# Modulation in eight products of 1024 columns, and four PSUM banks in the output projection and the early gates of a two-layer encoder

## The chip, the cores and the metric

The kernel runs on one core of a Trainium2 chip. What is measured is the time in device microseconds of one execution. Before the change it is 3258.42 us, the median of three runs (3254.71 to 3266.62 us). Five engines work side by side: TensorE (PE, with its weight loads shown apart as PEld), VectorE (DVE), ScalarE (ACT), GpSimd (POOL) and SyncE (SP), which here only starts transfers. Each works through its own list of instructions in order and waits for others by semaphores. Matrix products accumulate in PSUM banks; everything else lies in SBUF.

## What is computed

Two layers over 1024 tokens of width 1024, in float32. Each layer is a token mixer followed by a gated MLP with a short convolution. Six vectors of 1024 (shift, scale and gate for each half of a layer) come from the conditioning vector c; this is the modulation:

```python
c_act = jax.nn.silu(c)
for l in range(DEPTH):                               # 2 layers
    mod = (c_act @ w_mod[l] + b_mod[l])[:, None, :]  # w_mod[l]: 1024 x 6144
    sh1, sc1, g1, sh2, sc2, g2 = jnp.split(mod, 6, axis=-1)
    h = rms_norm(x, norm_g[l, 0]) * (1 + sc1) + sh1
    parts = jnp.split(h @ w_in[l], split_idx, axis=-1)
    ...                                              # four mixers A, B, C, D
    y = jnp.concatenate([oa, ob, oc, od], axis=-1) @ w_out[l]
    x = x + g1 * rms_norm(y, norm_g[l, 1])
    h = rms_norm(x, norm_g[l, 2]) * (1 + sc2) + sh2
    u = dwconv3(h @ w_up[l], ffn_conv[l])            # 1024 -> 2 x 2816
    ug, uv = jnp.split(u, 2, axis=-1)
    y = (jax.nn.gelu(ug, approximate=True) * uv) @ w_down[l]
    x = x + g2 * rms_norm(y, norm_g[l, 3])
```

## The kernel before

Activations lie transposed, with features on the 128 partitions and tokens along the free axis; the two token halves (512 each) are handled one after the other where PSUM asks for it. Every float32 operand is split into a high and a low part (ACT rounds, DVE or POOL subtracts, L110 and L111), and a product is made of three matmuls, high by high, high by low, low by high (mm3, L525 to L527). A program orders the instructions on each engine by the dependences and by the order of the code, and `issue_after` adds such an edge.

A layer runs through these stages.

- **Mixer**: projections and the four attention groups. PE is the busiest engine there; the change does not touch it.
- **Output projection** (`project_out`, L1149 to L1186). For each half of the tokens eight output tiles m, each 8 contraction tiles by three matmuls, into one PSUM bank of 128x512 and from there by ACT to y (L1173). After the first half, `between` puts in the residual and the MLP's input for that half (norm sums, modulated values on DVE and ACT, split). The second half takes all its banks from the pool pj, which has two.
- **Early gates** (`begin_early`, L1228): the part of six gate products that needs only the first half of the tokens, made while DVE, ACT and POOL bring the second half through its residual and norm. `begin` (L1215) makes eight plus four matmuls, ACT copies the bank out (L1221), twelve more are added to the same bank, and ACT copies again (L1225). All banks come from pj. The weight sums of the first two steps of the up projection (`sums`, L1236) are DVE work beside it.
- **Up projection** (`dense_up`, L1264): 22 steps, each with a convolution on DVE (L944, L946), a GELU on ACT (L1328), a product (L1329), and a store to `actd`. The four tiles ta, tb, tc, tn of the pool t4 hold the convolution's operands here.
- **Down projection** (`dense_down`, L1367). `whole` takes contraction tiles in groups of n (2 or 4), and for each of eight output tiles m makes 2 halves x n x 3 matmuls into a po tile (1024 columns) or two psc banks; DVE adds them to y (L1428). In the first group ACT copies instead. `some` does the last contraction tiles by token halves, 512 columns each (L1435).
- **Layer end**: norm sums, residual, and the next layer's modulated input.

The modulation of the first layer's last gate and five of the second layer's six vectors is a generator (`modulate`, L369) stepped by `advance` (L376). One step loads 128x512 of w_mod into one of two buffers (tag mr, L359) and adds its product with one column of c_act to an accumulator of 128x512 (tag mc, L362 or L364); 16 steps and a fold (`mod_fold`: two transposes, two reductions and some ten small instructions, L418 to L441) make one vector. Six such jobs are stepped in layer 0: 16 steps in the up projection (one per convolution step from the seventh on), 70 in the whole groups (three per m in groups of four, one in groups of two, none in the first group), and the 16 that are left over when `some` begins. In layer 1 the last gate is made in the whole groups.

Of the kernel before, what the change touches and what calls it, by code (L numbers as in the profile page):

```python
# [21 lines left out]
KT = 8  # L22
# [70 lines left out]
class Trunk:  # L93
# [252 lines left out]

    def mod_pieces(self, l, j, room=None):

        nc = self.nc
        accs = []  # L350
        for u in range(2):
            acc = room[u] if room else self.mc.tile([128, 512], F32, name="mc", tag="mc")
            for k in range(KT):
                if room:
                    w = room[2 + (8 * u + k) % (len(room) - 2)]
                else:
                    w = self.mr.tile([128, 512], F32, name="mr", tag="mr")
                at = 1024 * j + 512 * u
                nc.sync.dma_start(w, self.a["w_mod"][l, 128 * k:128 * k + 128, at:at + 512])  # L359
                s = self.cact[:, k:k + 1]  # L360
                if k == 0:
                    nc.vector.tensor_scalar(acc, w, s, None, op0=ALU.mult)  # L362
                else:
                    nc.vector.scalar_tensor_tensor(acc, w, s, acc, op0=ALU.mult, op1=ALU.add)  # L364
                yield
            accs.append(acc)
        return l, j, accs, 0

    def modulate(self, jobs):  # L369

        for l, j in jobs:
            part = yield from self.mod_pieces(l, j)
            self.mod_fold(part, self.mr.tile([128, 512], F32, name="mr", tag="mr"))
            yield

# [130 lines left out]
    def residual(self, y, l, g, hs, xsrc, dst, temp, adders=None, rs=None):  # L506
# [3 lines left out]
        for k in range(KT):  # L510
# [6 lines left out]
            nc.vector.scalar_tensor_tensor(yk, yk, self.col(l, g, k), rs, op0=ALU.mult, op1=ALU.mult)  # L517
            (nc.gpsimd if k % 2 else nc.vector).tensor_add(yk, yk, x)
            (nc.sync if dst is self.a["out"] else nc.scalar).dma_start(dst[128 * k:128 * k + 128, hs], yk)
# [357 lines left out]
    def modulations(self, l):  # L877

        tiles = [self.sp.tile([128, 2048], F32, name="room", tag=t) for t in ("s10", "s11")]
        room = [t[:, at:at + 512] for t in tiles for at in range(0, 2048, 512)]  # L880
        for j in (2, 4, 3):
            pieces = self.mod_pieces(l, j, room)
            try:
                while True:
                    next(pieces)
            except StopIteration as done:
                part = done.value
            yield
            self.mod_fold(part, room[2])
# [215 lines left out]
    def mixer(self, l):  # L1105
        tc, nc = self.tc, self.nc
        with ExitStack() as e:
# [29 lines left out]
            if l == 0:  # L1137
                self.mods = ExitStack()
                self.mc, self.mr = (p(n, 2, self.mods, side="right") for n in ("mc", "mr"))
            self.qlc, kls, rt, self.sc = self.open_shared(f"hmid{l}")  # L1140
# [4 lines left out]
    def project_out(self, l, y, between):  # L1145
        nc = self.nc
        order = ORDER_MIX
        with self.tc.tile_pool(name=f"wo{l}", bufs=1, reuse_waits="tile") as wo:
# [33 lines left out]
            for m in (2, 3, 4, 5, 0, 1, 6, 7):  # L1182
                products(1, (m,), (pj,), False)
                if m == 0:
                    between[1]()
# [28 lines left out]

    def begin(self, u, w1, between=None):  # L1215

        nc = self.nc
        b11, b21 = ([(self.hh[i][:, HALVES[0]], self.hl[i][:, HALVES[0]]) for i in range(k, k + 4)] for k in (0, 4))
        x = self.pj.tile([128, 512], F32, name="pj", tag="pj")
        self.quarter(x, w1, 0, b11)  # L1220
# [6 lines left out]
    def begin_early(self, l, ws):  # L1227

        nc, done = self.nc, []
        for t in range(self.ahead):  # L1230
            u = self.t4.tile([128, 1026], F32, name="u", tag=("tc", "tn")[t % 2])
            done.append(self.begin(u, ws[t] if t < len(ws) else self.up_weight(l, t)))
            nc.scalar.dma_start(self.kept[128 * t:128 * t + 128, :], u[:, 1:1025])
# [30 lines left out]
    def dense_up(self, l, early):  # L1264
# [10 lines left out]
        with tc.tile_pool(name=f"ux{l}", bufs=2, reuse_waits="tile") as ux, \  # L1275
# [79 lines left out]
            for t in range(2, FT):  # L1355
# [7 lines left out]
                gated(t, p.tail())  # L1363
                if t >= ahead:
                    self.advance(1)

    def dense_down(self, l, y, end):  # L1367
# [3 lines left out]
        with tc.tile_pool(name=f"dq{l}", bufs=4, reuse_waits="tile") as dq:  # L1371
# [3 lines left out]
            if last:  # L1375
                self.mc, self.mr = (right.enter_context(tc.tile_pool(name=f"{n}{l}", bufs=2, reuse_waits="tile",
                                                                     side="right")) for n in ("mc", "mr"))
                self.pieces = self.modulate([(l, 5)])
            pools = {"f": (self.fw, "uh", "ul"), "w": (self.w, "wh", "wl"), "q": (dq, "qh", "ql"), "p": (dp, "ph", "pl")}
# [33 lines left out]
            def whole(ops, first):  # L1413
                for m in range(8):
                    if m and not first:
                        self.advance(1 if len(ops) < 4 else 3)
                    if m % 3 < 2:
# [50 lines left out]
    def run(self):  # L1468
# [48 lines left out]
        for l in range(DEPTH):  # L1517
# [8 lines left out]
            with tc.tile_pool(name=f"fw{l}", bufs=3, reuse_waits="tile") as self.fw:  # L1526
                self.project_out(l, y, token_half(0, t))
                self.turn = cycle((0, 0, 0, 1, 1))
                self.pieces = self.modulate([(0, 5), (1, 1), (1, 0), (1, 2), (1, 4), (1, 3)] if l == 0 else [])
                with tc.tile_pool(name=f"te{l}", bufs=1, reuse_waits="tile") as self.te:  # L1530
                    early = [self.up_weight(l, t) for t in range(5)]
                    with tc.tile_pool(name=f"bd{l}", bufs=1, reuse_waits="tile", side="right") as bd:
                        t = self.temps(bd, x="few")
                        token_half(1, t)[0]()
                        done = self.begin_early(l, early)
                        early = [self.sums(l, k, False, self.t4) for k in range(2)]
                        self.dense_input(y, l, 1, t, adders[1], done)
# [91 lines left out]
```

## Time and profile before

| | before |
|---|---|
| median of three runs | 3258.42 us |
| profiled execution | 3276.93 us |
| its span in the trace | 3275.2 us |
| PE busy | 2909.4 us, 89% of the span |
| DVE busy | 2339.0 us, 71% |
| ACT, POOL busy | 1185.3 us, 36%; 1151.7 us, 35% |
| mean clock granted to PE | 0.95 of full speed |

PE is the engine to watch: where it waits, the time grows, and where it does not wait, other engines' work is hidden beside it. The share of each is an average over stages, so the stages are read apart. In layer 0 the output projection and early gates lie at 838 to 940 us of the span, the up projection from 1040 to 1390, the down projection's whole groups up to 1588 and its halves to 1670; in layer 1 the same stages begin at 2450, 2660 and 3000 us.

### The profile page before, as it was taken

Reading aid. Unit: us, or ns where it says so; the run is one execution under the profiler, and the core shown is the slowest. Engines: PE = TensorE matmul, PEld = TensorE weight load, DVE = VectorE, ACT = ScalarE, POOL = GpSimd, SP = SyncE. Lnnn points to the kernel's source line nnn. Section 1 sums busy time; section 2 is a strip of 40 time slices with the busy share of each in tenths; the row PEclk is TensorE's granted clock in tenths of the full one; section 3 lists DMA queues with packets and bytes.
Section 4 is the critical chain, followed back from the end, with each engine's and each line's share of the span. In section 5 each row is a group of like instructions: output and inputs, shape, how many; then the busy total and the mean of one; then the engine's idle time right before and its main releaser. Section 6 shows DMA issues by size and latency. Waiting matters only on the chain. (4 is left out here: it accounts for less than half of the span.)

```text
span 3275.2 us, 35394 instructions
## 1 busy us (share of the span) xinstructions
PE 2909.4 (89%) x13178; PEld 2299.8 (70%) x13178; DVE 2339.0 (71%) x3168; ACT 1185.3 (36%) x1702; POOL 1151.7 (35%) x797
## 2 busy tenths in 40 slices
PE   7888988988888999999888998898897799999897
PEld 3677767776656777777656787677675578877786
DVE  6687567697669778857776736578964797776456
ACT  4232443554443333321233333435534333334121
POOL 1221133224444444542332212242334445456131
PEclk8998999999999999999998999999998899999998
DMA  5235111102333222355531121110133232224323
GB/s 201 72 99 180 58 34 32 54 20 77 127 111 109 87 90 90 119 190 175 169 129 47 57 76 55 37 46 20 52 109 117 83 110 77 78 84 159 105 90 103
DMA packets 122680, 305.32 MB, mean 93 GB/s; under 512 B 13403, under 2 KB 32091, under 8 KB 122508
## 3 DMA queue, kind: packets, MB, share of 16 engines
q1 hardware_dynamic: 113868, 284.19, 26.5%
q10 hardware_dynamic: 8640, 18.88, 1.5%
q8 instruction: 103, 1.69, 0.2%
q14 instruction: 69, 0.57, 0.1%
HBM read 244.38 MB, written 62.03 MB: 94 GB/s over the span
## 5 line engine op out<-in xcount | busy, mean ns | idle before, releaser
L111 POOL TENSOR_TENSOR wl<-raw,wh 128x1024 fp32r<-128x1024 f32 (+2 forms) x82 | 203.3, 2481 | 470.5 <-ACT wh L110 273.0
L534 PE MATMUL pj<-hh,wh 128*128 128x512 f32 x800 | 329.4, 412 | 15.7 <-DVE ql L583 8.4
L535 PE MATMUL pj<-hl,wh 128*128 128x512 f32 x800 | 325.4, 407 | 10.2 <-POOL hl L461 6.4
L538 PE MATMUL pj<-hh,wl 128*128 128x512 f32 x800 | 208.8, 400 | 0.0
L534 PEld LDWEIGHTS pj<-hh,wh 128*128 128x128 f32 x800 | 155.6, 194 | 56.7 <-issue 15.6
L535 PEld LDWEIGHTS pj<-hl,wh 128*128 128x128 f32 x800 | 154.8, 194 | 52.3 <-POOL hl L461 10.2
L946 DVE SCALAR_TENSOR_TENSOR ta<-u,par,ta 128x1024 f32<-128x1024 f32 x88 | 154.9, 1761 | 34.2 <-ACT ta L942 34.1
L538 PEld LDWEIGHTS pj<-hh,wl 128*128 128x128 f32 x800 | 152.5, 192 | 35.5 <-issue 0.9
L698 PE MATMUL po<-s,v 128*96 128x128 f32 (+3 forms) x672 | 133.5, 363 | 44.1 <-ACT s L695 44.0
L698 PE MATMUL po<-hp,v 128*96 128x256 f32 x512 | 126.5, 403 | 37.1 <-ACT hp L695 36.7
L698 PEld LDWEIGHTS po<-s,v 128*96 128x96 f32 x672 | 101.3, 190 | 71.6 <-ACT s L695 54.7
L111 POOL TENSOR_TENSOR ul<-raw,uh 128x1024 fp32r<-128x1024 f32 x45 | 117.2, 2607 | 95.9 <-ACT uh L110 95.6
L110 ACT ACTIVATE wh<-raw 128x1024 fp32r<-128x1024 f32 (+2 forms) x90 | 94.1, 1045 | 154.5 <-PE pj L535 74.3
L581 ACT ACTIVATE qh<-pj 64x512 fp32r<-64x512 f32 x128 | 107.2, 838 | 98.4 <-PE pj L538 52.9
L583 DVE TENSOR_TENSOR ql<-pj,qh 64x512 fp32r<-64x512 f32 x64 | 55.4, 866 | 116.0 <-ACT qh L581 115.3
L946 DVE SCALAR_TENSOR_TENSOR tb<-u,par,tb 128x1024 f32<-128x1024 f32 x88 | 137.3, 1560 | 0.0
L698 PEld LDWEIGHTS po<-hp,v 128*96 128x96 f32 x512 | 85.9, 173 | 72.2 <-ACT hp L695 45.1
L111 POOL TENSOR_TENSOR pl<-raw,ph 128x1024 fp32r<-128x1024 f32 x26 | 67.9, 2612 | 178.0 <-issue 102.9
L364 DVE SCALAR_TENSOR_TENSOR mc<-mr,cact,mc 128x512 f32<-128x512 f32 x98 | 98.1, 1001 | 45.1 <-DMA mr<-in_w_mod_dram 44.7
L565 DVE TENSOR_TENSOR ks<-pj,ks 64x512 fp32r<-64x512 f32 x56 | 51.2, 914 | 108.7 <-ACT ks L564 108.0
L1428 DVE TENSOR_TENSOR y<-y,po 128x1024 f32<-128x1024 f32 x60 | 72.7, 1216 | 69.5 <-PE po L527 69.4
L685 PE MATMUL psc<-qh,ks 128*128 128x256 f32 (+2 forms) x272 | 88.2, 339 | 36.9 <-DVE s L813 15.2
(618 smaller groups left out, 8935.2 us busy)
## 6 DMA issues: line engine op xcount, KB each, us to landing
mr<-in_w_mod_dram SPq DMA_DIRECT2D x144, 256.0 KB, 3.1
raw<-in_w_up_dram SPq DMA_DIRECT2D x56, 512.0 KB, 3.7
raw<-in_w_in_dram SPq DMA_DIRECT2D x52, 512.0 KB, 3.4
raw<-in_w_down_dram SPq DMA_DIRECT2D x50, 512.0 KB, 3.7
actd<-ta SPq DMA_DIRECT2D x44, 512.0 KB, 2.6
uh<-in_w_up_dram SPq DMA_DIRECT2D x26, 512.0 KB, 3.8
room<-in_w_mod_dram SPq DMA_DIRECT2D x48, 256.0 KB, 3.8
xd<-y ACTq DMA_DIRECT2D x48, 256.0 KB, 4.0
```

The costliest lines, as they stand in the source:

```text
L110: self.nc.scalar.activation(hi, src, AF.Copy)
L111: (eng or self.nc.gpsimd).tensor_sub(lo, src, hi.bitcast(F32))
L364: nc.vector.scalar_tensor_tensor(acc, w, s, acc, op0=ALU.mult, op1=ALU.add)
L534: nc.tensor.matmul(ps, wh[:, ks], self.hh[k][:, hs], start=k == 0, stop=False, skip_group_check=True)
L535: nc.tensor.matmul(ps, wh[:, ks], self.hl[k][:, hs], start=False, stop=False, skip_group_check=True)
L538: nc.tensor.matmul(ps, wl[:, ks], self.hh[k][:, hs], start=False, stop=k == KT - 1, skip_group_check=True)
L581: nc.scalar.activation(self.perm(qh[h][o:o + 64], r)[:, n * half:n * half + n, :], src, AF.Copy)
L583: nc.vector.tensor_sub(lo, src, own.bitcast(F32))
L685: nc.tensor.matmul(ps, ks[:, c], qh[:, q0:q1], start=first, stop=False, skip_group_check=True)
L698: nc.tensor.matmul(o[0:96, co], v(tt, h), s[:, cs], start=co.start // 512 not in seen, stop=False, skip_group_check=True)
L946: nc.vector.scalar_tensor_tensor(o, t[:, i:i + n], cw(i), o, op0=ALU.mult, op1=ALU.add)
L1428: self.mark = nc.vector.tensor_add(d, d, p)
```

## The change

Five edits in one. The modulation runs in eight products of 1024 columns per vector instead of sixteen of 512, with one accumulator of 1024 columns, and its loads (512 KB instead of 256 KB) go into the four t4 tiles ta, tb, tc, tn, so the two mr buffers are gone. Up projection steps no longer advance it; its generator is made in the down projection, and a group of four advances it twice per m rather than three times. The second half of the output projection takes odd m from pj and even m from psc. The early gates alternate between pj and psc too. And the two early weight sums are ordered behind the last addition that the second half's residual makes on DVE.

```diff
-    def modulate(self, jobs):
+    def modulate(self, jobs, acc):
+        nc = self.nc
+        tags = cycle("abcn")
         for l, j in jobs:
-            part = yield from self.mod_pieces(l, j)
-            self.mod_fold(part, self.mr.tile([128, 512], F32, name="mr", tag="mr"))
-            yield
+            for k in range(KT):
+                w = self.tmp(next(tags))
+                nc.sync.dma_start(w, self.a["w_mod"][l, 128 * k:128 * k + 128, 1024 * j:1024 * j + 1024])
+                s = self.cact[:, k:k + 1]
+                if k == 0:
+                    nc.vector.tensor_scalar(acc, w, s, None, op0=ALU.mult)
+                else:
+                    nc.vector.scalar_tensor_tensor(acc, w, s, acc, op0=ALU.mult, op1=ALU.add)
+                yield
+            self.mod_fold((l, j, (acc[:, 0:512], acc[:, 512:1024]), 0), self.tmp(next(tags))[:, :512])
...
-            (nc.gpsimd if k % 2 else nc.vector).tensor_add(yk, yk, x)
+            if k % 2:
+                nc.gpsimd.tensor_add(yk, yk, x)
+            else:
+                self.added = nc.vector.tensor_add(yk, yk, x)
...
-                products(1, (m,), (pj,), False)
+                products(1, (m,), (pj if m % 2 else psc,), False)
...
-        x = self.pj.tile([128, 512], F32, name="pj", tag="pj")
+        x = (self.pj if bank == "pj" else self.psc).tile([128, 512], F32, name="x", tag=bank)
...
-            done.append(self.begin(u, ws[t] if t < len(ws) else self.up_weight(l, t)))
+            done.append(self.begin(u, ws[t] if t < len(ws) else self.up_weight(l, t), None, ("pj", "psc")[t % 2]))
...
                 gated(t, p.tail())
-                if t >= ahead:
-                    self.advance(1)
...
-                self.mc, self.mr = (right.enter_context(tc.tile_pool(name=f"{n}{l}", bufs=2, reuse_waits="tile",
-                                                                     side="right")) for n in ("mc", "mr"))
-                self.pieces = self.modulate([(l, 5)])
+                self.mc = right.enter_context(tc.tile_pool(name=f"mc{l}", bufs=1, reuse_waits="tile", side="right"))
+            self.pieces = self.modulate([(l, 5)] if last else [(0, 5), (1, 1), (1, 0), (1, 2), (1, 4), (1, 3)],
+                                        self.mc.tile([128, 1024], F32, name="mc", tag="mc"))
...
-                        self.advance(1 if len(ops) < 4 else 3)
+                        self.advance(1 if len(ops) < 4 else 2)
...
-                        early = [self.sums(l, k, False, self.t4) for k in range(2)]
+                        with self.queued(added):
+                            early = [self.sums(l, k, False, self.t4) for k in range(2)]
```

With 6 x 8 = 48 steps and 49 advances in layer 0's whole groups, all products and folds of layer 0 now lie there; nothing is left over for `some`.

How the order moves, at three places. First DVE in layer 0's first group of four contraction tiles. L362 and L364 are the products before (mc<-mr), L375 and L377 those after (mc<-ta, tb, tc, tn), L1428 and L1429 the additions to y. Before:

```order
L1428 TENSOR_TENSOR y<-y,psc 128x512
L364 SCALAR_TENSOR_TENSOR mc<-mr,cact,mc 128x512
L111 TENSOR_TENSOR ul<-ul,uh 128x1024
L364 SCALAR_TENSOR_TENSOR mc<-mr,cact,mc 128x512
L1428 TENSOR_TENSOR y<-y,psc 128x512
L364 SCALAR_TENSOR_TENSOR mc<-mr,cact,mc 128x512 x3
L1428 TENSOR_TENSOR y<-y,po 128x1024
L364 SCALAR_TENSOR_TENSOR mc<-mr,cact,mc 128x512 x2
L362 TENSOR_SCALAR mc<-mr,cact 128x512
L1428 TENSOR_TENSOR y<-y,po 128x1024
L364 SCALAR_TENSOR_TENSOR mc<-mr,cact,mc 128x512 x2
L1428 TENSOR_TENSOR y<-y,psc 128x512
```

After:

```order
L1429 TENSOR_TENSOR y<-y,po 128x1024
L377 SCALAR_TENSOR_TENSOR mc<-tc,cact,mc 128x1024
L377 SCALAR_TENSOR_TENSOR mc<-tn,cact,mc 128x1024
L1429 TENSOR_TENSOR y<-y,psc 128x512 x2
L377 SCALAR_TENSOR_TENSOR mc<-ta,cact,mc 128x1024
L111 TENSOR_TENSOR ul<-ul,uh 128x1024
L377 SCALAR_TENSOR_TENSOR mc<-tb,cact,mc 128x1024
L1429 TENSOR_TENSOR y<-y,po 128x1024
L377 SCALAR_TENSOR_TENSOR mc<-tc,cact,mc 128x1024
L377 SCALAR_TENSOR_TENSOR mc<-tn,cact,mc 128x1024
L1429 TENSOR_TENSOR y<-y,po 128x1024
```

Two products of 1024 columns now stand between the additions of two neighbouring m where three of 512 stood.

Second, DVE in layer 1's down projection, where the one job there is folded (L418 to L441 before, L423 to L446 after). Before:

```order
L418 STREAM_TRANSPOSE mr<-mc 128x512
L419 TENSOR_REDUCE sm<-mr 128x16
L418 STREAM_TRANSPOSE mr<-mc 128x512
L419 TENSOR_REDUCE sm<-mr 128x16
L421 COPY sm<-sm 64x32
L422 TENSOR_TENSOR sm<-sm 64x32
L423 COPY sm<-sm 32x32
L424 TENSOR_TENSOR sm<-sm 32x32
L426 COPY sm<-sm 32x8 x4
L432 TENSOR_TENSOR mod<-sm,par 128x8
L441 TENSOR_TENSOR gm<-mod,par 128x8
L1428 TENSOR_TENSOR y<-y,po 128x1024 x3
```

After:

```order
L1429 TENSOR_TENSOR y<-y,po 128x1024
L423 STREAM_TRANSPOSE ta<-mc 128x512
L424 TENSOR_REDUCE sm<-ta 128x16
L423 STREAM_TRANSPOSE ta<-mc 128x512
L1429 TENSOR_TENSOR y<-y,psc 128x512
L424 TENSOR_REDUCE sm<-ta 128x16
L426 COPY sm<-sm 64x32
L427 TENSOR_TENSOR sm<-sm 64x32
L428 COPY sm<-sm 32x32
L429 TENSOR_TENSOR sm<-sm 32x32
L431 COPY sm<-sm 32x8 x4
L1429 TENSOR_TENSOR y<-y,psc 128x512
```

The whole fold stood in one piece ahead of the next addition of a po tile; now additions stand within it.

Third, PE in layer 1's early gates (L1208, L1209, L1212 before; L1211, L1212, L1215 after; hx and hp are halves of the input, uh, ul, wh, wl split weights). Before, from the end of one gate's first part into the next:

```order
L1212 MATMUL pj<-hp,ul 128x512
L1208 MATMUL pj<-hp,uh 128x512 [waits Activation_49]
L1209 MATMUL pj<-hp,uh 128x512
L1208 MATMUL pj<-hp,uh 128x512
L1209 MATMUL pj<-hp,uh 128x512
L1208 MATMUL pj<-hx,uh 128x512
L1209 MATMUL pj<-hx,uh 128x512
```

After:

```order
L1215 MATMUL x<-hx,ul 128x512
L1215 MATMUL x<-hp,ul 128x512
L1211 MATMUL x<-hx,wh 128x512
L1212 MATMUL x<-hx,wh 128x512
L1211 MATMUL x<-hp,wh 128x512
L1212 MATMUL x<-hp,wh 128x512
```

...and, after the first matmuls of a further gate,

```order
L1212 MATMUL x<-hp,wh 128x512
L1215 MATMUL x<-hx,wl 128x512
L1211 MATMUL x<-hp,uh 128x512 [waits Activation_49]
L1212 MATMUL x<-hp,uh 128x512
L1211 MATMUL x<-hp,uh 128x512
L1212 MATMUL x<-hp,uh 128x512
```

The matmuls that wait for ACT's copy (pj<-hp,uh, now x<-hp,uh) now stand behind the first parts of two further gates (8+4 and 8+1 matmuls, 21 in all).

## Rows read from the trace of the kernel before

**Rows 1.** Page, busy time of each engine over the span.
```profile
PE 2909.4 (89%) x13178; PEld 2299.8 (70%) x13178; DVE 2339.0 (71%) x3168; ACT 1185.3 (36%) x1702; POOL 1151.7 (35%) x797
```

**Rows 2.** Windows by stage: us; PE, PEld, DVE, ACT, POOL busy; PEclk, DMA share, GB/s.
```profile
2450.00:2562.00 112.00, 82.88 (x293) 58.78 (x291) 53.22 (x82) 44.79 (x71) 43.65 (x31) 0.87 0.39 129
1062.00:1388.00 326.00, 313.12 (x1332) 249.96 (x1332) 267.86 (x251) 117.92 (x146) 161.80 (x123) 0.99 0.28 96
2685.00:2999.00 314.00, 310.07 (x1331) 250.56 (x1332) 242.87 (x235) 118.28 (x146) 159.61 (x123) 0.99 0.25 87
1402.00:1588.00 186.00, 167.38 (x701) 135.58 (x700) 135.58 (x174) 36.86 (x40) 67.11 (x29) 0.94 0.56 180
```

**Rows 3.** Waits of PE, 838 to 940 us: total, times, longest.
```profile
PE pw L525 <- ACT y L1173: 7.2, 2, 6.1
PE po L1348 <- ACT hx L110: 6.6, 1, 6.6
PE pj L1208 <- ACT u L1221: 4.0, 2, 2.5
```

**Rows 4.** Waits of PE, 2450 to 2562 us.
```profile
PE pj L1208 <- ACT u L1221: 10.0, 1, 10.0
PE pw L525 <- ACT y L1173: 8.8, 2, 5.9
```

**Rows 5.** Timeline of ACT, 861 to 879 us: start, duration, instruction, idle before.
```profile
869.29 1.06 ACT L1173 ACTIVATE y<-pw 128x512 f32<-128x512 f32 x2
...
877.56 0.60 ACT L1173 ACTIVATE y<-pw 128x512 f32<-128x512 f32 x1 [6.27 <-PE pw L527]
```

**Rows 6.** Windows of 7 us before and after one of PE's gaps.
```profile
1440.00:1447.00 7.00, 7.00 (x32) 5.80 (x31) 4.10 (x6) 1.06 (x1) 0.09 (x1) 1.00 0.49 147
...
1453.00:1460.00 7.00, 7.00 (x22) 5.53 (x22) 5.42 (x16) 0.87 (x1) 0.00 (x0) 0.67 0.70 228
```

**Rows 7.** GELU of the up projection, layer 0.
```profile
L1328 ACT ACTIVATE ta<-ta x17: 1048/1062/1064, 1061.7 to 1388.2; 128x1024 f32<-128x1024 f32 x17
```

**Rows 8.** GELU of the up projection, layer 1.
```profile
L1328 ACT ACTIVATE ta<-ta x17: 1049/1061/1065, 2684.7 to 2999.1; 128x1024 f32<-128x1024 f32 x17
```

**Rows 9.** Waits of PE in layer 0's whole groups, 1402 to 1588 us.
```profile
PE po L525 <- DVE y L1428: 18.6, 5, 6.5
```

**Rows 10.** Timeline of DVE, 1444 to 1454 us.
```profile
1447.91 1.97 DVE L364 SCALAR_TENSOR_TENSOR mc<-mr,cact,mc 128x512 f32<-128x512 f32 x1 [0.80 <-DMA mr<-in_w_mod_dram]
...
1451.26 1.21 DVE L1428 TENSOR_TENSOR y<-y,po 128x1024 f32<-128x1024 f32 x1
```

**Rows 11.** Lines of DVE, 1402 to 1588 us: busy, mean ns, idle before.
```profile
L364 DVE SCALAR_TENSOR_TENSOR mc<-mr,cact,mc 128x512 f32<-128x512 f32 x56 | 54.2, 968 | 29.9 <-DMA mr<-in_w_mod_dram 29.7
...
L362 DVE TENSOR_SCALAR mc<-mr,cact 128x512 f32<-128x512 f32 x8 | 8.7, 1082 | 1.8 <-DMA mr<-in_w_mod_dram 1.6
```

**Rows 12.** Durations (min/median/max) of a product, 512 columns.
```profile
L364 DVE SCALAR_TENSOR_TENSOR mc<-mr,cact,mc x98: 736/751/2892, 1106.0 to 3055.4; 128x512 f32<-128x512 f32 x98
```

**Rows 13.** Durations of the same operation on 1024 columns, in the convolution.
```profile
L946 DVE SCALAR_TENSOR_TENSOR ta<-u,par,ta x88: 1269/1274/3474, 982.5 to 2995.7; 128x1024 f32<-128x1024 f32 x88
```

**Rows 14.** Waits of PE, 1588 to 1670 us, layer 0's `some`.
```profile
PE pd L525 <- DVE y L1435: 7.2, 4, 2.5
```

**Rows 15.** Timeline of DVE, 3055 to 3070 us, layer 1.
```profile
3056.07 0.70 DVE L418 STREAM_TRANSPOSE mr<-mc 128x512 f32<-128x512 f32 x1
...
3065.08 2.35 DVE L1428 TENSOR_TENSOR y<-y,po 128x1024 f32<-128x1024 f32 x2
```

**Rows 16.** Waits of SP's queue, 1402 to 1588 us.
```profile
SPq L359 <- DVE mc L364: 59.0, 49, 3.5
```

**Rows 17.** Page: POOL's split of a loaded weight; that load, KB, us to landing.
```profile
L111 POOL TENSOR_TENSOR pl<-raw,ph 128x1024 fp32r<-128x1024 f32 x26 | 67.9, 2612 | 178.0 <-issue 102.9
...
raw<-in_w_down_dram SPq DMA_DIRECT2D x50, 512.0 KB, 3.7
```

More of the change, by code (lines that the diff above doesn't have):

```diff
@@ L345, in rotary, with mod_sum @@
                 nc.sync.dma_start(self.csd[:, 512 * i:512 * i + 512], cs)
-    def mod_pieces(self, l, j, room=None):
+    def mod_sum(self, l, j, room):
         nc = self.nc
@@ L351, in mod_pieces @@
         for u in range(2):
-            acc = room[u] if room else self.mc.tile([128, 512], F32, name="mc", tag="mc")
+            acc = room[u]
             for k in range(KT):
[L354 to L357, printed above, removed]
+                w = room[2 + (8 * u + k) % (len(room) - 2)]
                 at = 1024 * j + 512 * u
@@ L364, in mod_pieces @@
                     nc.vector.scalar_tensor_tensor(acc, w, s, acc, op0=ALU.mult, op1=ALU.add)
-                yield
             accs.append(acc)
         return l, j, accs, 0
-    def modulate(self, jobs):
+    def modulate(self, jobs, acc):
+        nc = self.nc
+        tags = cycle("abcn")
         for l, j in jobs:
-            part = yield from self.mod_pieces(l, j)
-            self.mod_fold(part, self.mr.tile([128, 512], F32, name="mr", tag="mr"))
-            yield
+            for k in range(KT):
[8 more added lines that the diff above has]
+            self.mod_fold((l, j, (acc[:, 0:512], acc[:, 512:1024]), 0), self.tmp(next(tags))[:, :512])
     def advance(self, n):
@@ L881, in modulations @@
         for j in (2, 4, 3):
[L882 to L887, printed above, removed]
+            part = self.mod_sum(l, j, room)
             yield
@@ L1138, in mixer @@
                 self.mods = ExitStack()
-                self.mc, self.mr = (p(n, 2, self.mods, side="right") for n in ("mc", "mr"))
+                self.mc = p("mc", 1, self.mods, side="right")
             self.qlc, kls, rt, self.sc = self.open_shared(f"hmid{l}")
@@ L1213, in quarter, with begin @@
         return mm
-    def begin(self, u, w1, between=None):
+    def begin(self, u, w1, between=None, bank="pj"):
         nc = self.nc
         b11, b21 = ([(self.hh[i][:, HALVES[0]], self.hl[i][:, HALVES[0]]) for i in range(k, k + 4)] for k in (0, 4))
-        x = self.pj.tile([128, 512], F32, name="pj", tag="pj")
+        x = (self.pj if bank == "pj" else self.psc).tile([128, 512], F32, name="x", tag=bank)
         self.quarter(x, w1, 0, b11)
@@ L1528, in run @@
                 self.turn = cycle((0, 0, 0, 1, 1))
-                self.pieces = self.modulate([(0, 5), (1, 1), (1, 0), (1, 2), (1, 4), (1, 3)] if l == 0 else [])
                 with tc.tile_pool(name=f"te{l}", bufs=1, reuse_waits="tile") as self.te:
@@ L1534, in run @@
                         token_half(1, t)[0]()
+                        added = self.added
                         done = self.begin_early(l, early)
-                        early = [self.sums(l, k, False, self.t4) for k in range(2)]
+                        with self.queued(added):
+                            early = [self.sums(l, k, False, self.t4) for k in range(2)]
                         self.dense_input(y, l, 1, t, adders[1], done)
```

## The prediction

> **What bounds the kernel now.** I first read the busy time per engine: PE works 89% of the span [rows 1], so time can only be won where PE waits or runs at a lower clock. Second came the windows by stage [rows 2]. In layer 1's output projection and early gates PE is busy 82.9 of 112 us. In layer 0's whole groups of the down projection it is busy 167.4 of 186 us, and DVE 135.6. In layer 0's up projection it is busy 313.1 of 326 us, and in layer 1's, which is the same work without the modulation's steps, 310.1 of 314. Third came PE's waits in these stages. In both layers the second half of the output projection waits for ACT to empty a bank (7.2 and 8.8 us), the early gates wait for ACT's first copy (4.0 and 10.0 us), and the transition ends with 6.6 us of waiting for the input's second half [rows 3, 4], in layer 1 by a row that reads the same as that of layer 0. In the whole groups of layer 0 PE waits 18.6 us in five pieces for DVE's additions to y [rows 9]. The clock adds to each long wait: in 7 us just before a gap PE ran 32 matmuls at a granted clock of 1.00, in 7 us after it 22 at 0.67, a mixture of the two levels, 1.2 and 2.4 GHz [rows 6]. At 7.00 / 32 = 0.219 us per matmul the ten missing ones are 2.2 us. I add 2.2 us to a wait of about 5 us or more.
>
> **Part 1, the banks (term A).** The timeline shows why ACT is late [rows 5]: it makes the first half's modulated values and splits, and two copies out of PSUM stand behind them and run together at 869.3 us. With two banks PE stops; then the last copy, at 877.6 us, waits 6.27 us for PE. With four banks PE can finish two further tiles, 2 x 24 x 0.219 = 10.5 us of work, which covers the longest wait of 6.1 and 5.9 us. So the last copy can come about 7 us earlier in layer 0 and 8 us in layer 1, with the clock. What is late next is the chain from this last copy over the residual and norm of the second half to the split input, on which PE already waits 6.6 us at the end. That chain begins when the last copy ends, so it moves by as much; it does not get shorter. For that reason I do not credit all of the gates' 4.0 and 10.0 us: in the order, 21 matmuls (21 x 0.219 = 4.6 us) now go ahead of the waiting ones, but what PE gains there it can lose at the end's 6.6 us. I take 8 us for layer 0 and 10 for layer 1, 18 in all. The ends are 6 (the chain does not follow) and 7.2 + 8.8 + 4.0 + 10.0 + 3 x 2.2 = 36.6. The order of the weight sums behind the residual's last addition costs nothing while the residual is on that chain and the sums are not needed until the up projection; if they came late, two steps of it would wait, which is in term F.
>
> **Part 2, no steps in the up projection (term B).** The removed work there is 16 products, 16 loads and a fold. GELU runs 17 times between the first and last start in each layer: 1061.7 to 1388.2 in layer 0 [rows 7], 2684.7 to 2999.1 in layer 1 [rows 8], 326.5 against 314.4 us. The 12.1 us is what layer 0 pays over layer 1, and its DVE is busy 267.9 against 242.9 us [rows 2]. Part may be other differences of the layers, so I take 9, with ends 0 and 12.
>
> **Part 3, layer 0's whole groups (term C).** Before, three steps of 512 columns stand between the additions of neighbouring m; after, two of 1024. A product of 512 columns takes 736 ns at best, 751 in the median [rows 12] and 968 in the mean of this stage [rows 11], so 0.22 us of each is blocking. On 1024 columns the trace has the same operation in the convolution: 1269 ns at best, 1274 in the median, 3474 at most [rows 13]. If blocking is paid once per instruction, a wide product is 1.27 + 0.22 = 1.49 us and 48 of them 71.5 us; if it grows with length, 1.27 x 968 / 751 = 1.64 us and 78.6 us. The 64 narrow ones took 54.2 + 8.7 = 62.9 [rows 11]. One more fold lies in this stage, about 5 us (its four wide parts at 0.7 us and ten small ones). DVE goes from 135.6 to between 149 and 156 us, against PE's 167.4. It fits, with 11 to 18 us to spare over some 35 tiles, half a microsecond each. What also goes is the waiting for loads: DVE idles 29.9 us ahead of these products with two buffers [rows 11], and the addition that releases PE stands behind them (a product that waited 0.80 us for its load and then took 1.97 us, then a transpose and a reduction, then the addition at 1451.3) [rows 10]. With four buffers a load of 3 to 4 us is asked for three products ahead. So most of the five waits go, but a blocked product can still make an addition late. I take 13 us, about half of 18.6 + 3 x 2.2 = 25.2. The ends are -6 and 25.
>
> A page of the Trainium skill bears on the blocking: "SBUF — State Buffer", section "SBUF: two separate sides", says that VectorE and GpSimd share a port pair as an exclusive lock for a whole instruction, so that the loser stops outright. By that rule the first of the two forms would hold, 71.5 us, not 78.6. The spread of one shape from 736 to 2892 ns [rows 12] looks like a lock, but does not tell which form it takes on twice the length.
>
> **Part 4, layer 0's halves (term D).** The 16 leftover steps and a fold stand in front of additions there; PE waits 7.2 us in four pieces for them [rows 14]. All of this work leaves the stage. I take 7 (3 to 12, the upper end with clock for two of the waits).
>
> **Part 5, layer 1 (term E).** The fold stands in one piece on DVE from 3056.07 to 3065.08, and only then come the additions [rows 15]; PE waits as long. After, additions stand between its parts. Of 9.0 + 2.2 I take 9 (3 to 11).
>
> **What is added (term F).** In layer 0's whole groups the modulation's loads grow from 64 x 256 KB to 48 x 512 KB, 8.4 MB more. At 180 GB/s for a share of 0.56 [rows 2], 321 GB/s at full share, that is 26 us more on DMA, and the share becomes (104 + 26) / 172 = 0.76. Loads of weights stand in SP's list behind loads that wait for their buffer; before, SP already waits 59.0 us for DVE to free one [rows 16]. The first loads also wait now until the convolution's last steps leave ta and tb. I take 4 us of loss, ends 0 and 12.
>
> **The sum.** 18 + 9 + 13 + 7 + 9 - 4 = 52 us off the profiled execution's 3276.9: 3224.9. The median is 3258.42 / 3276.93 = 0.9944 of the profiled time, so 3207 us.
>
> **The rivals.**
> 1. The chain sets the transitions. ACT and DVE, not the banks, fix when the second half is ready, and A is 6 instead of 18: a gain of 40, 3219 us. For it speaks the 6.6 us at the end of both layers; against it that ACT idled 6.27 us for PE ahead of its last copy.
> 2. DVE is too full in layer 0's whole groups, so C is -6: a gain of 33, 3226 us. For it speaks the half microsecond of slack per tile; against it the 29.9 us of idleness that four buffers take away.
> 3. The change does not do what it says: the waits of A, C and E move to other places and the 12.1 us are the layer's own. With a quarter of 52 left, 3246 us. Against it speaks that the waits lie in five separate stages.
> 4. Slower. In layer 0 the weights of the next group are asked for behind the wide loads. Preparing a group of four exposed costs 8 loads of 512 KB at 321 GB/s, 13 us, and half of the 4 x 2.6 us of POOL's splits [rows 17], about 19 with a clock loss. Four such boundaries are 76 us; with C gone, 3276.9 - 39 + 76 = 3314, or 3295 us. It decides from (39 + 16) / 4 = 14 us per boundary on. Against it: before, with SP just as often held, the list shows no wait of PE for such a split in that stage: the additions are its only row [rows 9].
>
> **How the numbers follow.** Forecast 0.60, rivals 0.15, 0.12, 0.08 and 0.05. About 0.5%, 16 us, is what a measurement can tell from no change. Forecast and rivals 1 and 2 are faster by more (0.87); rival 3 is the same, and I put 0.08 on it; slower keeps 0.05. The likeliest case's own range comes from the terms between their ends, a gain of 30 to 79: 3180 to 3229. The whole range runs to 3240, which takes in rivals 1 and 2 with some loss.
>
> **What would show it.** Right: the waits on L1173's copies gone in both layers and the last copy 7 to 8 us nearer to the first; 314 to 318 us between GELU's ends in layer 0; DVE 149 to 156 us busy in its whole groups, with PE's wait there under 10 us; no fold in front of an addition at layer 1's first groups. Wrong: as much PE waiting at the end of the transition as was saved before it, wide products of 2 us in the mean, or PE waiting for splits of down-projection weights.

## The result, and the profile after

The changed kernel takes 3207.8 us (median of four runs, 3207.2 to 3212.5) against 3259.0 before; the ratio is 0.9844, with a 95% interval of 0.9823 to 0.9864, and 0.9850 (0.9834 to 0.9865) when it was run again. The forecast was 3207. The total came out right with two of its terms wrong: term A gained next to nothing in layer 0 (from 1 us lost to 2 won), where 8 us were forecast, and term D about 16 us instead of 7.

The page after, busy time per engine, answers to [rows 1]; the windows by stage have the columns of [rows 2]. In order they are the transition of layer 0 and of layer 1, the up projection and the whole groups of layer 0.

```profile
PE 2882.4 (90%) x13178; PEld 2283.3 (71%) x13178; DVE 2314.6 (72%) x3112; ACT 1183.9 (37%) x1702; POOL 1162.4 (36%) x797
```

```profile
838.00:943.00 105.00, 82.35 (x303) 57.38 (x302) 60.20 (x86) 44.95 (x72) 44.89 (x27) 0.94 0.43 147
2398.00:2508.00 110.00, 91.21 (x336) 64.83 (x334) 63.12 (x93) 47.16 (x76) 48.71 (x34) 0.92 0.44 153
1064.00:1380.00 316.00, 311.19 (x1332) 250.52 (x1332) 245.46 (x238) 118.86 (x147) 159.95 (x125) 0.99 0.27 90
1394.00:1568.00 174.00, 161.63 (x683) 130.77 (x683) 154.27 (x170) 34.47 (x38) 69.02 (x27) 0.97 0.65 225
```

In the whole groups DVE works more, 154.3 us of a shorter stage, and the mean clock rose from 0.94 to 0.97. PE's waits there (total, times, longest) fell from 18.6 us [rows 9] to 10.5, just above the 10 that the prediction named, with a new kind behind it, for a split of activations on DVE:

```profile
PE po L533 <- DVE y L1429: 10.5, 3, 4.8
PE po L534 <- DVE pl L111: 1.6, 1, 1.6
```

DVE's products there, by line and buffer (count, busy us, mean ns, idle before), answer to [rows 11]: 42 in these rows, 65.1 us, 1.55 us each, and the idle time ahead of them, 31.7 us before, is 1.8. The six first products of a vector (L375) are not among the 42.

```profile
L377 DVE SCALAR_TENSOR_TENSOR mc<-tc,cact,mc 128x1024 f32<-128x1024 f32 x11 | 17.1, 1557 | 0.1
L377 DVE SCALAR_TENSOR_TENSOR mc<-tb,cact,mc 128x1024 f32<-128x1024 f32 x10 | 16.6, 1662 | 1.4 <-DMA tb<-in_w_mod_dram 1.2
L377 DVE SCALAR_TENSOR_TENSOR mc<-tn,cact,mc 128x1024 f32<-128x1024 f32 x11 | 16.1, 1466 | 0.2
L377 DVE SCALAR_TENSOR_TENSOR mc<-ta,cact,mc 128x1024 f32<-128x1024 f32 x10 | 15.3, 1526 | 0.1
```

In layer 0's transition the wait for a bank of the output projection, 7.2 us [rows 3], is gone, and the wait for the norm's squares has grown by as much. Before, it was:

```profile
PE po L158 <- ACT sq L165: 1.8, 1, 1.8
```

After:

```profile
PE po L158 <- ACT sq L165: 8.8, 4, 4.5
PE po L1351 <- ACT hx L110: 6.5, 1, 6.5
PE x L1211 <- ACT u L1224: 4.1, 2, 2.5
```

In layer 1's [rows 4] the gates' wait fell from 10.0 to 5.7 us, the bank's wait of 8.8 went, and the squares' rose from 3.1 to 4.9:

```profile
PE x L1211 <- ACT u L1224: 5.7, 1, 5.7
PE po L158 <- ACT sq L165: 4.9, 2, 2.6
```

### The profile page after: what moved, and what is told of

Its sections match the earlier page's. It is cut to its first block, busy times and chain, and to the rows that moved or that the text cites. A ratio compares the mean times of both kernels' runs of the same rounds, so it can differ in the third digit from the quotient of the medians.

```text
span 3205.6 us, 35206 instructions
## 1 busy us (share of the span) xinstructions
PE 2882.4 (90%) x13178; PEld 2283.3 (71%) x13178; DVE 2314.6 (72%) x3112; ACT 1183.9 (37%) x1702; POOL 1162.4 (36%) x797
## 5 line engine op out<-in xcount | busy, mean ns | idle before, releaser
L542 PEld LDWEIGHTS pj<-hh,wh 128*128 128x128 f32 x800 | 154.8, 194 | 55.2 <-issue 16.2
L1429 DVE TENSOR_TENSOR y<-y,po 128x1024 f32<-128x1024 f32 x60 | 72.9, 1216 | 70.0 <-PE po L535 70.0
L693 PE MATMUL psc<-qh,ks 128*128 128x256 f32 (+2 forms) x272 | 86.3, 333 | 36.2 <-DVE s L821 15.2
L533 PE MATMUL po<-ph 128*128 128x512 f32 x240 | 95.3, 397 | 7.8 <-DVE y L1429 4.8
```

Of the source, the lines that this page charges most:

```text
L533: nc.tensor.matmul(ps, wh, xh, start=first, stop=False, skip_group_check=True)
L542: nc.tensor.matmul(ps, wh[:, ks], self.hh[k][:, hs], start=k == 0, stop=False, skip_group_check=True)
L693: nc.tensor.matmul(ps, ks[:, c], qh[:, q0:q1], start=first, stop=False, skip_group_check=True)
L1429: self.mark = nc.vector.tensor_add(d, d, p)
```

## The experiments

To see where the time goes I read, in every trace, the times of the same landmarks and took the length of each stage between them. T is the transition (first copy of the output projection to the first matmul of the up projection), U the up projection (sixth to last GELU), W the whole groups (last GELU to DVE's last addition there), E the end of layer 0 (from there to the first rounding of the next layer's queries), each from start to start; 0 and 1 are the layers. All in us:

| kernel | T0 | U0 | W0 | E0 | T1 | U1 | W1 | span |
|---|---|---|---|---|---|---|---|---|
| before, second trace | 142.6 | 327.1 | 198.9 | 161.2 | 150.0 | 315.1 | 200.8 | 3267.6 |
| changed, first trace | 143.3 | 315.2 | 187.7 | 145.5 | 140.6 | 313.2 | 192.3 | 3205.6 |
| changed, second trace | 140.5 | 316.0 | 190.3 | 145.0 | 142.3 | 312.7 | 193.8 | 3211.5 |
| modulation only | 142.1 | 318.0 | 188.6 | 148.1 | 152.2 | 314.5 | 192.1 | 3226.1 |
| narrow, moved | 141.8 | 316.7 | 198.9 | 168.1 | 152.6 | 314.2 | 199.8 | 3272.7 |
| two buffers | 142.9 | 317.2 | 206.2 | 145.1 | 146.4 | 312.4 | 195.4 | 3240.0 |
| output banks undone | 143.3 | 316.2 | 190.3 | 145.5 | 146.0 | 313.8 | 192.3 | 3221.8 |
| gate banks undone | 142.8 | 316.3 | 190.5 | 145.5 | 147.1 | 313.2 | 192.5 | 3225.3 |
| sums' order undone | 139.7 | 316.6 | 193.5 | 146.0 | 145.9 | 314.6 | 192.2 | 3220.0 |
| squares first | 133.5 | 317.9 | 190.9 | 145.7 | 139.5 | 313.8 | 192.6 | 3204.6 |
| squares first, again | 138.0 | 315.8 | 193.7 | 147.9 | 140.7 | 313.0 | 192.1 | 3204.7 |
| both norms first | 135.8 | 315.1 | 192.8 | 144.9 | 140.3 | 312.9 | 192.0 | 3204.1 |
| products in the halves | 140.6 | 314.9 | 188.1 | 151.6 | 139.7 | 313.2 | 192.3 | 3212.2 |

**The kernel before, once more.**

> The kernel before, unchanged, for a second profile of it. Its first profiled execution took 3276.9 us, 18 above its median, and the changed kernel's 3207.4, its median, so 70 us lie between the two traces where the medians differ by 51. Theory: the 18 us are chance in stages that the change does not touch or touches little; a second profile near 3259 then shows 320 to 327 us between the sixth and the last GELU of layer 0 and a wait of 15 to 20 us for additions in layer 0's whole groups, as the first did, and is shorter elsewhere. Rival: the first profile was long just in the stages of the change; then the up projection of layer 0 is near 316 and the whole groups' wait near 10 in the second one, and terms B and C were read off an unusual execution.

All stages of the change repeat within 1 us of the first trace but for two: W0 was 201.7 and T1 153.1 there. U0 is 327.1 and PE's wait for additions in the whole groups 18.6 us again. So terms B and C were read off a usual execution, and the rival falls; the theory that the 18 us lay elsewhere by chance is not shown either: of the 7.6 us between the two spans, W0 and T1 make 5.9, and the medians of this one kernel differ by up to 15 us between the groups of runs (3259, 3272, 3274 and 3261 us). Times are therefore compared as ratios to the kernel before within a group.

**Modulation only.** The banks' and the sums' lines set back to those of the kernel before.

> The changed kernel with the banks and the order of the sums set back to what they were: only the modulation is changed. Theory: the banks gain nothing in layer 0 and about 12 us in layer 1, as the landmarks of the two traces say; this kernel is then about 12 us slower than the changed one, 3220 us, and its layer 1 transition (last copy of the output projection to first matmul of the up projection) is as before. Rival: the banks gain 18 us as forecast and something else lost 7 in layer 0; then 3226. Second rival: the modulation makes all of the 51 us and this kernel stays at 3208.

0.9877 (0.9862 to 0.9891) of the kernel before. The modulation makes 1.2 of the 1.6%, and the rest of the change is worth about 0.3% or 9 to 11 us (0.9850 and 0.9844 beside this, each from its own group), near the 12 of the first theory: T1 is 152.2 against 140.6 and 142.3, while T0 is as in the changed kernel.

**Narrow products, moved.**

```diff
-                if t >= ahead:
-                    self.advance(1)
...
-                        self.advance(1 if len(ops) < 4 else 3)
+                        self.advance(2 if len(ops) < 4 else 4)
```

> The kernel before with its products of 512 columns and two load buffers, but no step in the up projection, and four per tile in groups of four, two in groups of two, in the down projection. Theory: width and buffers pay, not the move; a narrow step costs DVE (62.9 + 31.7 us of waiting) / 64 = 1.45 us, so 96 of them and the 72.7 us of other work are 212 us against the 186 of layer 0's whole groups before: that stage grows by 20 to 30 us, the up projection gains 11, the halves 10 to 18, and the whole is 3250 to 3260. Rival: the move alone makes the gain in layer 0, and the time is 3259 - 35 = 3224 or less.

0.9987 (0.9972 to 1.0001). U0 falls by 10.4 us and E0 rises by 6.9. W0 does not grow at all, which the expectation had wrong: the whole groups took only some of the added steps, and 22 products of L364 start after their last addition, where the kernel before has 14. So the move by itself carries most of the cost to the end of the layer, and the time does not show a gain.

**Two of the four buffers.** `cycle("abcn")` becomes `cycle("ab")`.

> The changed kernel with two of the four load buffers (ta and tb in turn). Theory: the four buffers hide the loads; with two, a product of 1.5 us waits for a load of 3 to 4 us that could only start when the product two before had ended, so DVE waits 1 to 2 us for each of 48 and layer 0's whole groups take 180 to 200 us again instead of 174: 3220 to 3240. Rival: the width alone pays, since two wide loads carry as many bytes ahead as four narrow ones: then it stays within 4 us of 3208.

0.9900 (0.9879 to 0.9922), against 0.9844. W0 is 206.2 instead of 187.7 and 190.3. DVE's rows show why, 28.8 us idle before the products where the changed kernel has 1.8:

```profile
L377 DVE SCALAR_TENSOR_TENSOR mc<-tb,cact,mc 128x1024 f32<-128x1024 f32 x21 | 33.2, 1582 | 13.6 <-DMA tb<-in_w_mod_dram 13.4
L377 DVE SCALAR_TENSOR_TENSOR mc<-ta,cact,mc 128x1024 f32<-128x1024 f32 x21 | 29.7, 1414 | 15.2 <-DMA ta<-in_w_mod_dram 15.1
```

W0 alone does not tell what width is worth, for here all 48 products lie in it, where the narrow ones moved have 71 of their 96 there and the rest in E0. W0 and E0 together are 367.0 us with the narrow products moved, 351.3 with wide ones and two buffers, 333.2 and 335.3 with four (and 360.1 before, where 15 narrow products run in the up projection). So width with two buffers, each of them twice as large, gains 16 us there, and the two further buffers 16 to 18 more.

**Squares first.** One more edge on ACT:

```diff
+                self.squared = nc.scalar.activation(sq, t, AF.Square)
...
-                        with self.queued(added):
+                        with self.queued(added), self.queued(squared):
```

> The changed kernel with one more edge: ACT's first instructions of the two early weight sums stand behind the last square of the second half's first norm. In the changed kernel's layer 0 that norm takes 14.0 us from the last copy to the end of its sums where it took 8.8, and one ACT instruction, the rounding of a loaded weight (v<-raw), waits 2.70 us there for its load with three squares behind it; POOL's subtraction for it stands ahead of POOL's part of the sum. Theory: this queue on ACT and POOL is what gave back the banks' 5 to 6 us in layer 0; with the edge the norm's sums take 9 to 10 us again, the first matmul of the up projection comes 4 us earlier in layer 0, and the time is 0.1 to 0.15% below the changed kernel's. Rival: PE or the low clock sets the sums, and nothing moves by more than 1 us. Layer 1 has no such wait: 0 to 0.6 us there under both.

The transition has two norms of the second half, the residual's (the first) and that of the MLP's input (the second); in each ACT squares, PE and POOL add the squares up, and DVE transposes the sums. In the changed kernel ACT's list reads, in layer 0 (start, duration, instruction, idle before):

```profile
872.31 0.59 ACT L1176 ACTIVATE y<-pw 128x512 f32<-128x512 f32 x1
...
875.16 0.63 ACT L165 ACTIVATE sq<-y 128x512 f32<-128x512 f32 x1 [0.70 <-PE po L158]
878.48 0.63 ACT L110 ACTIVATE v<-raw 128x512 fp32r<-128x512 f32 x1 [2.70 <-DMA raw<-in_w_up_dram]
879.02 1.13 ACT L165 ACTIVATE sq<-y 128x512 f32<-128x512 f32 x2
881.71 0.63 ACT L165 ACTIVATE sq<-y 128x512 f32<-128x512 f32 x1 [1.56 <-POOL acc L173]
```

and DVE can transpose the finished sums only at 886.88. The load that ACT waits for was issued late, just after POOL had ended its split of a weight in the same pool of buffers:

```profile
872.54 2.37 POOL L111 TENSOR_TENSOR wl<-raw,wh 128x1024 fp32r<-128x1024 f32 x1
...
874.94 0.33 SPq L1245 DMA_DIRECT2D raw<-in_w_up_dram  x1
```

With the edge, ACT:

```profile
870.07 0.59 ACT L1176 ACTIVATE y<-pw 128x512 f32<-128x512 f32 x1
...
875.80 0.63 ACT L165 ACTIVATE sq<-y 128x512 f32<-128x512 f32 x1 [0.41 <-POOL acc L173]
...
877.33 0.62 ACT L110 ACTIVATE v<-raw 128x512 fp32r<-128x512 f32 x1
```

and DVE:

```profile
879.51 0.72 DVE L178 STREAM_TRANSPOSE t<-po 128x512 f32<-128x512 f32 x1 [11.85 <-PE po L158]
```

From the end of the last copy to this transposition it is 8.85 us in every trace of a kernel with two banks in the output projection, except for 9.6 where the gates have four; 13.0 to 15.2 us in the six traces with four banks in the output projection and no edge; and 8.8 in all three with the edge. So the place of the rounding in ACT's list is what made the norm longer in layer 0. The ratio was 0.9817 (0.9790 to 0.9844).

**The banks apart.** The line of `products`, or that of `begin_early`, as before.

> The changed kernel with the second half of the output projection on two banks again; the early gates keep four. Theory: in layer 1 the banks of the output projection are what moves the last copy by 9 us, and with two the last copy there comes 6 to 9 us later and the up projection 6 to 9 us later; in layer 0 the last copy comes 5 to 6 us later and the up projection at the same time within 1 us, since its norm waits for the load of a weight anyway. Time 7 to 9 us above the changed kernel's. Rival: the gates' banks carry the gain in layer 1 (their wait was the longest, 10.0 us); then this kernel is within 3 us of the changed one.

> The changed kernel with the early gates on two banks again; the output projection keeps four. Theory: the gates lie beside the chain of residual and norm, which ends with PE waiting 6.5 us for the split input in both layers; so their banks are worth 0 to 3 us, with PE's wait for the first copies in layer 1 near 10 us again. Rival: they carry half of layer 1's gain, and this kernel is 5 us or more slower than the changed one.

0.9845 (0.9813 to 0.9876) and 0.9852 (0.9825 to 0.9880), which tells nothing against 0.9844 from another group. In their own group the medians, 3222.3 and 3223.0 us, lie 7 above the 3215.6 of the kernel without the sums' order (below), which has all the banks, but the runs overlap. The traces tell more, if T1 is taken apart, for with the same code there it lies anywhere from 139.7 to 146.4 us (the kernel with two buffers has the latter). Without the output banks layer 1's time from the first copy to the last is 81.7 us, against 74.3 to 77.1 in all kernels that have them: 5 to 7 us, the low end of what was expected, and T0 does not move. Without the gate banks PE waits 9.4 us for the first copy there instead of the 5.5 to 6.1 of the kernels with all banks, and from the first norm's transposition to the second's it is 57.1 us, like the 55.9 to 57.8 of the other four traces with two banks there, against 49.2 to 54.3 in the nine with four. So the gates' banks are worth some 3 to 7 us of this stretch, more than the theory's 0 to 3, though T1 itself, 147.1, is only just outside the spread above. The squares' sums of the second norm stand among and behind the gates in PE's own list, so a gate that waits can put off the chain; this last step is read from the order and was not tested by itself.

**The order of the sums.** `if True:` for `with self.queued(added):`.

> The changed kernel without the order of the sums behind the residual's last addition. Theory: one subtraction and one addition of 0.7 to 1.8 us on DVE change places, and the time is the same within 2 us; only in the second norm of the transition does it show, by at most 1 us per layer. Rival: the chain is so tight that each layer loses the 1.8 us.

0.9832 (0.9804 to 0.9860). T1 is 145.9, inside the spread just named, so a worth of this edge is not shown. T0 is 139.7, 3.6 us under the changed kernel's first trace, and 3.3 of these are the second norm. In layer 0 it takes, from transposition to transposition, 47.5 to 47.8 us in four traces and 41.4 to 46.0 in the others. In just those four two of DVE's instructions of the second sum are held up, and PE's longest wait for a square is 4.4 to 4.5 us, against at most 2.8 elsewhere. Here they are in the changed kernel, with POOL's split of another weight, and then without the edge:

```profile
922.54 1.79 DVE L1261 TENSOR_TENSOR raw<-wh,raw 128x512 f32<-128x512 f32 x1
924.26 2.82 DVE L1262 TENSOR_TENSOR raw<-wh,wl 128x512 f32<-128x512 f32 x1
...
923.86 2.68 POOL L111 TENSOR_TENSOR ul<-wl,uh 128x1024 fp32r<-128x1024 f32 x1
```

```profile
922.58 0.68 DVE L1261 TENSOR_TENSOR raw<-wh,raw 128x512 f32<-128x512 f32 x1
923.18 0.68 DVE L1262 TENSOR_TENSOR raw<-wh,wl 128x512 f32<-128x512 f32 x1
...
923.89 2.34 POOL L111 TENSOR_TENSOR ul<-wl,uh 128x1024 fp32r<-128x1024 f32 x1 [1.40 <-ACT uh L110]
```

In the first, POOL's split is under way when the second subtraction comes and ends at 926.54, half a microsecond before it; in the second, both subtractions are over when the split starts.

**One group to compare: the changed kernel, squares first, both norms first, products in the halves.** The third kernel makes the second sum after `dense_input`, with its edges behind `added` and that norm's last square. The edit of the fourth:

```diff
-                        self.advance(1 if len(ops) < 4 else 2)
+                        self.advance((0 if not last else 1) if len(ops) < 4 else 2)
...
+                    if not last and hs == HALVES[0]:
+                        self.advance(1)
```

> The changed kernel again, on the same chip as the three that follow, to measure them against it. Theory and rival alike: 0.984 to 0.985 of the kernel before.

> The kernel with ACT's part of the early weight sums behind the first norm's last square, again, beside the changed kernel on one chip. Theory: it starts layer 0's up projection 5 to 7 us earlier (the rest of the 9.8 us seen between the two first traces was two DVE instructions of the sums that were held up, 1.79 and 2.82 us for 0.68) and ends 4 to 8 us earlier. Rival: the 0.27% between the two ratios was the chips; then the two are within 3 us.

> As the one before, and the second early weight sum is put behind the squares of the second norm too (its instructions on DVE behind the residual, on ACT behind the last square of the input's norm). Theory: in the second norm three squares wait on ACT behind two roundings of that sum, which wait for a load (2.0 to 3.5 us); without them PE's wait for squares there (3 to 7 us) goes, and each layer's up projection starts 2 to 3 us earlier: 4 to 6 us less than the kernel with the first edge alone. Rival: the sum is then late for the up projection, which waits for its third weight set, and the gain is lost or turns into 1 to 5 us of loss.

> The changed kernel with layer 0's last six products and last fold taken out of the group of two tiles and put between the additions of the first halves, one per tile, as the kernel before had its leftovers there. Theory: the 13 us that the end of layer 0 lost (from the last addition of the whole groups to the first rounding of the next layer's queries, 161 us before, 148 after) was DVE time of such products among the halves' additions; six wide ones of 1.5 us and a fold of 5 give back 6 to 12 us of it, and the whole groups gain at most 3. Rival: it was the two small buffers, whose loads held SP's list ahead of the second half's; with four buffers the end stays within 2 us of the changed kernel's.

The ratios are 0.9850 (0.9834 to 0.9865), 0.9832 (0.9815 to 0.9849), 0.9821 (0.9807 to 0.9834) and 0.9833 (0.9819 to 0.9848). Squares first repeats its norm of 8.85 us; T0 is 2.5 us shorter than the changed kernel's, less than the 5 to 7 expected, with a long second norm in both traces (47.5 and 47.7 us). Its median, 3207.4, is 3.6 us lower, and the intervals overlap: a gain in time over the changed kernel is not shown. By its median, 3203.0 us, both norms first is the fastest of all, 8 us under the changed kernel's 3211.0, and the two intervals just touch. Its second norm is 6 us shorter than in squares first, again, but PE then waits longer for the split input, so T0 kept a third of that:

```profile
PE po L1351 <- ACT hx L110: 10.8, 1, 10.8
```

Products in the halves lengthen E0 by 6.6 us and shorten W0 by 2.2, as the theory had it, with four buffers. (The 148 us of that expectation are those of modulation only; the changed kernel has 145.) The time does not show the loss: its median, 3205.3 us, is below the changed kernel's, and the intervals overlap.

## Why the prediction was right, and where it was not

- **Term A, 18 us: about 10 came, nearly all in layer 1.** The step that failed is "that chain begins when the last copy ends, so it moves by as much". In layer 0 the last copy came 6 to 8 us earlier after the first, and the first norm got longer by 4 to 5, because the list of ACT holds a weight's rounding among the squares and its load was no earlier than before; the second norm, where it was held up, took 2 more. In layer 1 the same rounding waited 0.9 us at most, T1 fell from 150.0 to 153.1 us (four traces with the old banks) to 140.6 and 142.3, by 8 to 12 us, and 10 were forecast; the gates' part of that was larger than I allowed.
- **Term B, 9 us: 11 to 12.** The difference between the layers was the modulation, nearly all of it: U0 is 315 to 316 us now, beside U1's 313, and moving the narrow steps away is enough for 10.4. The fold that the prediction counts among the removed work was not there: no fold runs in that stage of the first trace.
- **Terms C and F, 13 - 4 = 9 us: 9 to 11 off W0.** DVE's busy time, 149 to 156 us forecast, is 154.3. F has its place: DVE's first addition comes later after the last GELU, in layer 0 at 23.8 us in the changed kernel's first trace against 21.6 and 19.0 in the two traces before, in layer 1 at 24.1 against 20.4 and 20.3. With narrow products moved it is 20.3 and 20.4, and all kernels with wide loads have 23.7 us or more. Two w_mod loads stand among the group's first loads in SP's list there; that they are the cause was not tested.
- **Term D, 7 us: 16.** I priced the 7.2 us that PE waited for additions [rows 14] and left out what else stood behind the leftovers in DVE's list: the sums of the layer end's first norm. The end of that norm, DVE's transposition of its sums, before (second trace) and after:

```profile
1637.01 0.72 DVE L178 STREAM_TRANSPOSE tn<-po 128x512 f32<-128x512 f32 x1 [1.28 <-PE po L158]
```

```profile
1601.85 0.72 DVE L178 STREAM_TRANSPOSE tn<-po 128x512 f32<-128x512 f32 x1 [1.28 <-PE po L158]
```

  From the last addition of the whole groups that is 48.3 us before and 34.8 after (49.3 and 33.7 in the other two traces); from there to the end of E0 it is 113 and 111. So 14 of the 16 us are gained by the time of this norm. About half of that are the first half's additions, whose last one comes 7 us earlier; behind it, before, the last transposition and reduction of the fold and its small instructions stand among the norm's sums. Seven loads also hold SP for 12.5 us ahead of the second half's activations:

```profile
1609.60 12.47 SPq L359 DMA_DIRECT2D mr<-in_w_mod_dram  x7
1623.96 0.33 SPq L1196 DMA_DIRECT2D uh<-actd  x1
```

  but that load moves by less than 5 us, from 35.2 us behind the last addition of the whole groups to 30.7. Six wide products and a fold in the halves cost 6.6 of the 16 us with four buffers, and this norm then comes at 39.0. What SP's list adds was not tested by itself.
- **Term E, 9 us: 7 to 9** off W1. PE's wait at the fold (second trace before; the first puts the same gap, 8.8 us, down to a rounding on ACT) is gone after:

```profile
PE po L525 <- DVE y L1428: 9.1, 1, 9.1
```

The sum by the second traces is T0 2.1 + T1 7.7 + U0 11.1 + W0 8.6 + E0 16.2 + W1 7.0 = 52.7, where the forecast had 52. Terms A and D missed by 8 to 9 us each, in opposite directions, so the agreement to the microsecond is luck. Rivals 2 to 4 did not happen; rival 1 was true of layer 0 alone, where, as one of the signs of being wrong has it, PE waited as much longer for the squares as it waited less for a bank.

On the blocking: the mean of a wide product in layer 0's whole groups is 1.47 to 1.60 us in the eleven traces with them, 0.19 to 0.32 over its median of 1.28, and that of a narrow one 0.96 to 1.12 in three traces, 0.21 to 0.37 over its median of 0.75. So an instruction of twice the length is held no longer, which speaks for the first form; the 1.49 and 1.64 us of the two forms alone, both near the changed kernel's 1.55, would not tell. In the first traces 12 of the 57 narrow products are held by more than 0.1 us and 8 of the 42 wide ones, and each of these has an instruction of POOL beside it; of the others, 4 of 45 and 5 of 34 have one. The rule of the Trainium skill, "SBUF — State Buffer", section "SBUF: two separate sides", that the pair is locked for a whole instruction, agrees with that in this stage.

## What to carry to other kernels

Freeing banks shortens a stage that ends with a wait only if nothing else in the lists of the engines on the new path waits for something that has not moved: look for loads' roundings among the chain's instructions, and order the chain first. Work that is stepped beside a busy stage needs enough load buffers that no step waits for its load; with two, the wide products here waited 28.8 us for loads and their stage was 7 us longer than before, with four they waited 1.8 and it was 9 to 11 shorter. Leftover work at a layer's end can cost more than the waits that name it, here 16 us against 7, since the next norm stands behind it in the same engine's list and the next layer's start behind that.

## What the runs showed of the hardware

The same DVE subtraction of 512 columns took 0.68 us in some traces of a place and 2.82 in others, with the same order on DVE; in the long case a split on POOL was already under way, in the short one it started afterwards. Layer 0's second norm took 44.2 us in one trace of squares first and 47.5 in the other, the one with such an instruction. And T1 spread by 7 us between kernels with the same code there; why is not shown.
